# Hybrid decoder layer: all of GpSimd's DMA additions for weight sums issued in the projections, whole, at 0.75 for each weight load, and none beside the attention pairs

## The chip, the cores and the metric

The kernel runs on one core of a Trainium2 chip. Its time is the device time of one execution in microseconds (us). The engines go by the profile's names: PE is TensorE (matmuls; PEld is its weight loading), DVE is VectorE, ACT is ScalarE, POOL is GpSimd, SP is SyncE, which here only issues DMAs.

## The reference

One layer of a decoder trunk, in float32: an RMS norm, one wide input projection whose columns feed three token mixers (gated DeltaNet, GLA, forgetting attention), SiLU gates on each, one output projection with a residual, and a last norm.

```python
def hybrid_layer(x, norm_w, w_in, ...):
    h = rms_norm(x, norm_w)
    proj = (jnp.pad(h, ((0, 0), (PAD, 0), (0, 0))) @ w_in)      # 2048 -> 7585 columns
    (dq, dk, dv, dz, db, da, gq, gk, gv, gz, gl, fq, fk, fv, fz, ff) = split_cols(proj)
    o_dn = gated_head_norm(gated_delta_rule_chunked(...), dz, dn_norm_w)    # 6 heads x 128
    o_gla = gated_head_norm(gla_chunked(...), gz, gla_norm_w)               # 5 heads
    o_fox = forgetting_attention(fq, fk, fv, log_f) * silu(fz)              # 5 heads x 128
    return x + jnp.concatenate([o_dn, o_gla, o_fox], -1) @ w_out
```

There are 512 tokens and 16 meta tokens (528 in all), and the model is 2048 wide.

## The kernel before, in words

**Projections.** Each block of 128 output columns has a weight of 2048 x 128, which is loaded in two halves of 128 x 1024 (512 KB). `load_half` (L144) issues the load on SP's queue into `raw`; ACT casts it to a high part `whi` (L170), DVE subtracts to get the low part `wlo` (L171), and PE multiplies `whi` with the high and low parts of the activations and `wlo` with the high part (L245). `raw`, `whi` and `wlo` have two buffers each, so the loads run about two halves ahead of PE. Blocks come in the order: DeltaNet group 0 (keys, values, queries), DeltaNet group 1, GLA gates, GLA heads, the first attention head; between them stand the small matmuls of the mixers, placed in PE's order by hand.

**Pairs.** For attention heads 1 to 4 most blocks are computed two at a time, by `inproj_pair`: a Strassen-Winograd scheme with seven products (L580) in place of eight. It needs sums and differences of weights. The output projection of the first ten heads does the same in its products (L1410).

**Weight sums by DMA.** The sums are made in DRAM scratch, `ti` (seven input pairs) and `tw` (five output pairs), by DMAs alone. For each pair four copies ("moves") put a weight half into scratch: one move goes out on SP's queue in each `load_half` behind the weight load (L149). Then four additions per pair, DMAs with `accum_op=add` that GpSimd issues, add another weight or an earlier sum to it. Twelve pairs make 48 moves and 48 additions. Additions are generators in the list `chores`: first two for each pair that add a weight to a move (`ti<-in_w_in`, `tw<-in_w_dn`), then one for each pair that adds sum 0 to copy 1, then one that adds sum 1 to copy 3 (`ti<-ti`, `tw<-tw`); the input pairs come before the output pairs. How many go out is set in `load_half`:

```python
        due[0] += rate[0]                  # L156; due starts at -6
        while due[0] > 0 and chores:
            cost = next(chores[0], None)   # issues one addition (or half of one)
            if cost is None:
                chores.pop(0)
            else:
                due[0] -= cost
```

`AHEAD` (L1294) sets the rate. From the first DeltaNet block on it is 0.55 additions for each weight half. At attention head 1, where the pairs begin, it becomes 0.26, and there an addition is cut into two halves of 64 partitions (L494), each with a semaphore wait for the newest `wlo` subtraction on DVE; in the projections it is whole (L499) and only ordered behind the newest cast.

**Order.** A scheduler sets each engine's order when the program is built, from these dependencies and priorities. POOL's queue also holds the clamp of every SiLU (L390), the masks (L702, L726, L1225), memsets and products of the mixers, and 24 loads of the activations for the pairs (L535, L536, L555). An instruction on POOL starts only when all ahead of it have been issued.

**The inverse of a DeltaNet group** (`dn_inverse`) is a chain that passes POOL and three DMA trips: POOL clears `ab` (L739), ACT's queue loads it from scratch (L747, L748), POOL sets its diagonal (L751), DVE does 58 dependent steps (L756, L758), ACT's queue writes it out (L761, L762) and loads it turned (`iv`, L765, `xm`, L767), DVE transposes blocks (L771), and PE multiplies (`pm`, L777) at a place that is fixed in its order. ACT copies the transposed blocks into `uf`, which POOL clears at L793.

Of the kernel before, what the change touches and what calls it, by code (L numbers as in the profile page):

```python
# [14 lines left out]
ALU = mybir.AluOpType  # L15
# [3 lines left out]
P = 128  # L19
# [63 lines left out]
def tile_hybrid_trunk(ctx, tc, xT, xtok, mtok, w_gate, w_in, w_out, w_dn, consts, lmask, fin_w, out, dbg=None):  # L83
# [19 lines left out]
    V, A, G, PE = nc.vector, nc.scalar, nc.gpsimd, nc.tensor  # L103
# [71 lines left out]
    pace, splits, heads_, waits = [None, None], [], [], []  # L175

    def paced(*ins):

        for x in ins:
            tc.add_manual_dep(x.ins, pace[x.ins.engine == pace[1].engine].name, mybir.DependencyInfo(  # L180
                mybir.DependencyClass.NoSync, mybir.DependencyReason.DATA), reason="paced")
# [16 lines left out]
    def part(name, n=512):  # L198
        return hp.tile([P, T], F32R, tag="x", name=name)[:, :n]
# [29 lines left out]
    head = {}  # L229
# [259 lines left out]
    def steps_of(jobs):  # L489

        for out_, in_ in jobs:
            if ("pair", 0) in head:
                for s in (slice(0, 64), slice(64, P)):
                    x = G.dma_start(out=out_[s], in_=in_[s], accum_op=ALU.add, max_dma_last_dim=2048)  # L494
                    tc.add_manual_dep(x.ins, pace[1].name, mybir.DependencyInfo(
                        mybir.DependencyClass.Sync, mybir.DependencyReason.DATA), reason="paced")
                    yield 0.5
            else:
                paced(G.dma_start(out=out_, in_=in_, accum_op=ALU.add, max_dma_last_dim=2048))  # L499
                yield 1  # L500

    def in_jobs(n):
        h, one, two = PAIRS[n]
# [11 lines left out]
    def jobs(*groups):  # L515

        for g_ in groups:
            moves.extend(dict(out=o, in_=i) for o, i in g_[0])
        for st in range(1, 4):
            for g_ in groups:  # L520
                chores.append(steps_of(g_[st]))
# [769 lines left out]
            nc.sync.dma_start(out=zd[DN_HEADS + GLA_HEADS + h], in_=z)  # L1291


    AHEAD = {(0, -1): (0.55, (-1, -2, -3, -4, -5, -6, -7), (0, 1, 2, 3, 4)), ("f", 1): (0.26,)}  # L1294
    XSUM = {1: (0, 1, 2), 2: (3, 4, 5), 3: (6, 7)}
    MIX = 10
    PM, SP = (308, 340), (8, 11)
# [1 line left out]
    def ahead(g, i):  # L1299
        for n in AHEAD.get((g, i), ()):  # L1300
            if isinstance(n, tuple):
                jobs(*[in_jobs(-k - 1) if k < 0 else out_jobs(k) for k in n])
            else:
                rate[0] = n
# [133 lines left out]
    def weigh(tb, cc):  # L1438
        return G.tensor_tensor(out=acc[tb, cc], in0=acc[tb, cc], in1=fw[cc], op=ALU.mult)  # L1439
# [119 lines left out]
    for c in range(4):  # L1559
        f = part(f"fw{c}").bitcast(F32)  # L1560
# [16 lines left out]
    for cc in range(3):  # L1577
        for tb in range(4):
            x = weigh(tb, cc)
# [4 lines left out]
    for tb in range(4):  # L1584
# [25 lines left out]
        for cc in (1, 0, 3, 2):  # L1610
# [5 lines left out]
            else:  # L1616
                V.tensor_scalar_mul(a, a, r)
            (nc.scalar if tb == 3 and cc == 2 else nc.sync).dma_start(
                out=out[tb * P : (tb + 1) * P, cc * 512 : (cc + 1) * 512], in_=a)
# [60 lines left out]
```

## Time and profile before

| | |
|---|---|
| median of 3 runs | 987.03 us (986.32 to 987.07) |
| the profiled execution | 986.87 us, its span 985.2 us, 1.67 us outside it |
| granted TensorE clock | 0.997 |
| busy in the span | PE 975.0 us, DVE 670.5, ACT 480.3, POOL 218.2 |

Busy times come from the instructions' records; a wait is put down to the instruction that ended it. "L499" is line 499 of the kernel before. A row of the DMA list gives the issuing queue, how often, the size, and the median time from issue to landing.

### The profile page before, as it was taken

To read this page: it belongs to the slowest core of one execution; us is meant where nothing else is said; L and a number is where in the kernel's file an instruction comes from. 1 tells how busy PE (TensorE), PEld (TensorE's weight loads), DVE (VectorE), ACT (ScalarE), POOL (GpSimd) and SP (SyncE) were. 2 spreads that over 40 slices of the span, in tenths; PEclk is the share of its full clock that TensorE was granted. 3 is DMA by queue.
4 is the path that set the end of the run, shared out by engine and by line. 5 is a ranking of instruction groups with operands and counts; after the bars stand their busy time and mean duration, and the time that the engine had idled before them with its cause. 6 is when DMAs were issued, how large, how long until landed. Compare 5 with 4: busy or idle time off the path is not lost.

```text
span 985.2 us, 19830 instructions
## 1 busy us (share of the span) xinstructions
PE 975.0 (99%) x7762; PEld 894.4 (91%) x7762; DVE 670.5 (68%) x1462; ACT 480.3 (49%) x1051; POOL 218.2 (22%) x237
## 2 busy tenths in 40 slices
PE   9999999999999999999999999999999999999996
PEld 7899999899999888899899988899999998888885
DVE  5457886975657985334685847867767768987665
ACT  7753534344456334234546445655555545644345
POOL 0021322222123334201213122333322120000033
PEclk9999999999999999999999999999999999999998
DMA  9835598887458787644646666677766588366534
GB/s 345 303 119 206 161 251 222 238 257 224 127 164 221 212 252 191 164 112 102 154 138 161 158 153 194 190 218 218 195 200 171 174 267 296 132 214 212 186 115 172
DMA packets 70339, 191.83 MB, mean 195 GB/s; under 512 B 14077, under 2 KB 17325, under 8 KB 69476
## 3 DMA queue, kind: packets, MB, share of 16 engines
q1 hardware_dynamic: 46048, 152.53, 45.2%
q0 software_dynamic: 15104, 31.66, 18.4%
q10 hardware_dynamic: 9092, 6.36, 2.4%
q8 instruction: 61, 1.00, 0.4%
q14 instruction: 34, 0.28, 0.1%
HBM read 179.84 MB, written 60.88 MB: 244 GB/s over the span
## 4 chain that ended last, share of the span: by engine, by line
PE 98%; DVE 1%; ACT 1%; issue 0%; POOL 0%; DVEq 0%; ACTq 0%; POOLq 0%
PE pp L245 49%; PE pp_a L580 8%; PE pq L1410 6%; PE pp L314 5%; PE pa L1410 3%; PE ps L1410 3%; PE pt L1410 2%; PE pp_b L580 2%; PE pp_d L580 2%; PE pp_c L580 2%; PE pr L1410 1%; PE pss L1059 1%; PE pgate L431 1%; PE pfo L1285 1%; PE pfa L1237 1%; PE pg L723 1%
## 5 line engine op out<-in xcount | busy, mean ns | idle before, releaser
L245 PE MATMUL pp<-xl,whi 128*128 128x264 f32 (+2 forms) x1120 | 273.9, 306 | 0.0
L245 PE MATMUL pp<-xh,whi 128*128 128x264 f32 (+2 forms) x1120 | 272.9, 306 | 0.0
L245 PE MATMUL pp<-xh,wlo 128*128 128x264 f32 (+2 forms) x1120 | 272.2, 305 | 0.0
L170 ACT CAST whi<-raw 128x1024 fp32r<-128x1024 f32 x131 | 137.2, 1047 | 180.2 <-PE pp L245 125.1
L171 DVE TENSOR_TENSOR wlo<-raw,whi 128x1024 fp32r<-128x1024 f32 x131 | 162.8, 1243 | 66.4 <-ACT whi L170 56.0
L245 PEld LDWEIGHTS pp<-xl,whi 128*128 128x128 f32 x1120 | 182.7, 189 | 9.1 <-issue 0.4
L245 PEld LDWEIGHTS pp<-xh,whi 128*128 128x128 f32 x1120 | 182.3, 189 | 9.2 <-issue 0.2
L245 PEld LDWEIGHTS pp<-xh,wlo 128*128 128x128 f32 x1120 | 182.8, 189 | 8.5 <-issue 0.2
L390 POOL TENSOR_SCALAR stc<-cv 128x528 f32<-128x528 f32 (+1 forms) x18 | 28.1, 1563 | 145.8 <-DVE cv L622 136.2
L622 DVE SCALAR_TENSOR_TENSOR cv<-pb,cpk,cv 128x528 f32<-128x528 f32 (+1 forms) x54 | 41.1, 760 | 0.8
L1439 POOL TENSOR_TENSOR acc<-acc,fw 128x512 f32<-128x512 f32 x4 | 6.1, 1542 | 138.9 <-DVE wll L171 138.9
L170 ACT CAST whis<-raws 128x1024 fp32r<-128x1024 f32 x20 | 20.7, 1049 | 28.0 <-PE ps L1410 9.7
L171 DVE TENSOR_TENSOR wlos<-raws,whis 128x1024 fp32r<-128x1024 f32 x20 | 24.2, 1222 | 14.8 <-ACT whis L170 14.8
L580 PE MATMUL pp_a<-t,whi 128*128 128x264 f32 (+1 forms) x224 | 30.3, 283 | 0.0
L580 PEld LDWEIGHTS pp_a<-t,whi 128*128 128x128 f32 x224 | 28.0, 188 | 0.4
L580 PE MATMUL pp_a<-xh,whi 128*128 128x264 f32 x112 | 28.1, 286 | 0.0
L580 PE MATMUL pp_a<-xl,whi 128*128 128x264 f32 x112 | 27.9, 285 | 0.0
L379 DVE TENSOR_TENSOR pb<-pp,rstd 128x264 f32<-128x264 f32 (+1 forms) x36 | 13.8, 421 | 17.3 <-PE pp L245 17.3
L1410 PE MATMUL pq<-whia,a 128*128 128x512 f32 x80 | 25.4, 393 | 0.0
L1410 PE MATMUL ps<-whis,s 128*128 128x512 f32 x80 | 25.4, 394 | 0.0
L1410 PE MATMUL pq<-whis,s 128*128 128x512 f32 x80 | 25.4, 394 | 0.0
L390 POOL TENSOR_SCALAR stdz<-zdz 128x512 f32<-128x512 f32 x6 | 11.2, 1877 | 63.2 <-DVE zdz L408 62.2
(506 smaller groups left out, 2111.4 us busy)
## 6 DMA issues: line engine op xcount, KB each, us to landing
raw<-in_w_in SPq DMA_DIRECT2D x103, 512.0 KB, 3.6
ti<-in_w_in SPq DMA_DIRECT2D x28, 512.0 KB, 5.3
raw<-ti SPq DMA_DIRECT2D x28, 512.0 KB, 3.7
tw<-in_w_dn SPq DMA_DIRECT2D x20, 512.0 KB, 5.2
raws<-tw SPq DMA_DIRECT2D x15, 512.0 KB, 4.3
ti<-in_w_in POOLq DMA_DIRECT2D x14, 512.0 KB, 6.0
ti<-ti POOLq DMA_DIRECT2D x14, 512.0 KB, 7.0
tw<-in_w_dn POOLq DMA_DIRECT2D x10, 512.0 KB, 6.9
```

Of the source, the lines that this page charges most:

```text
L170: pace[0] = A.copy(hi, raw).ins
L171: pace[1] = V.tensor_tensor(out=lo, in0=raw, in1=hi.bitcast(F32), op=ALU.subtract).ins
L245: mm = PE.matmul(p_[:, :nt], wt[:, j * m : (j + 1) * m], xx[k][:, t0 : t0 + nt], start=(k == 0 and wt is hi and xx is xh), stop=(k == KT - ...
L314: mm = PE.matmul(ps[:, :S], wt[:, j * P : (j + 1) * P], xx[k][:, NM:T], start=(k == 0 and wt is hi and xx is xh), stop=(k == KT - 1 and wt ...
L379: V.tensor_tensor(out=o, in0=p_[rows], in1=rstd[rows, t0 : t0 + n], op=ALU.mult)
L390: maxes.append(G.tensor_scalar_max(t, src, LOW).ins)
L431: PE.matmul(pgate[a][:, :HT], wg[k // 8][:, k % 8, :], xx[k][:, a * HT : (a + 1) * HT], start=(k == 0 and xx is xh), stop=(k == KT - 1 and ...
L580: m = PE.matmul(p_[:, cols], wt[:, j * P : (j + 1) * P], xx[j][part_][:, cols], start=first and i == 0, stop=i == len(todo) - 1, skip_grou ...
L622: V.scalar_tensor_tensor(out=c, in0=pb[:, t0 + w : w + T], scalar=cwc[:, blk, w : w + 1], in1=c, op0=ALU.mult, op1=ALU.add)
L723: PE.matmul(pg[:r, j * r : (j + 1) * r], kT[:, j, ts], kT[:, j, ts], start=True, stop=True)
L1059: mm = PE.matmul(ps[o0 : o0 + n, b * n : b * n + n], kx[rr, k0 : k0 + n], qx[rr, q0 : q0 + n], start=True, stop=True)
L1410: mm = PE.matmul(p_, o_[:, s], w_, start=(first and n == 0), stop=(last and n == 2), skip_group_check=True)
```

## The change

The branch of `steps_of` that cuts an addition in two beside the pairs goes; every addition is whole and only ordered, not made to wait. The rate is 0.75 from the first DeltaNet block on, and the rate for the pairs is gone.

```diff
     def steps_of(jobs):
         for out_, in_ in jobs:
-            if ("pair", 0) in head:
-                for s in (slice(0, 64), slice(64, P)):
-                    x = G.dma_start(out=out_[s], in_=in_[s], accum_op=ALU.add, max_dma_last_dim=2048)
-                    tc.add_manual_dep(x.ins, pace[1].name, mybir.DependencyInfo(
-                        mybir.DependencyClass.Sync, mybir.DependencyReason.DATA), reason="paced")
-                    yield 0.5
-            else:
-                paced(G.dma_start(out=out_, in_=in_, accum_op=ALU.add, max_dma_last_dim=2048))
-                yield 1
+            paced(G.dma_start(out=out_, in_=in_, accum_op=ALU.add, max_dma_last_dim=2048))
+            yield 1
...
-    AHEAD = {(0, -1): (0.55, (-1, -2, -3, -4, -5, -6, -7), (0, 1, 2, 3, 4)), ("f", 1): (0.26,)}
+    AHEAD = {(0, -1): (0.75, (-1, -2, -3, -4, -5, -6, -7), (0, 1, 2, 3, 4))}
```

The order of PE's instructions is the same in both programs; those of SP, ACT and DVE differ by two or three instructions that change places with a neighbour. POOL's order differs throughout. Lines behind L500 are seven lower in the changed kernel (L499 is L492 there).

POOL around the inverse of DeltaNet group 0, before (`stc` and `stdz` are SiLU clamps, `ab` the inverse's buffer):

```order
L390 TENSOR_SCALAR stc_1652<-cv_1647 128x528
L499 DMA ti<-in_w_in 256x512
L390 TENSOR_SCALAR stc_1792<-cv_1787 128x512
L739 MEMSET ab_2052 51x1024
L499 DMA ti<-in_w_in 256x512
L390 TENSOR_SCALAR stc_1919<-cv_1914 128x512
L751 MEMSET ab_2052 51x32
L499 DMA ti<-in_w_in 256x512
```

The same place now:

```order
L390 TENSOR_SCALAR stc_1654<-cv_1649 128x528
L492 DMA ti<-in_w_in 256x512
L390 TENSOR_SCALAR stc_1795<-cv_1790 128x512
L492 DMA ti<-in_w_in 256x512
L732 MEMSET ab_2056 51x1024
L492 DMA ti<-in_w_in 256x512
L390 TENSOR_SCALAR stc_1922<-cv_1917 128x512
L744 MEMSET ab_2056 51x32
L492 DMA ti<-in_w_in 256x512
```

One more addition stands ahead of the memset of `ab`.

POOL some 40 us later, before (`stdz` the clamp of a gate, `uf` the inverse's result, `pb` a border of the convolution, `b` a block buffer of the inverse):

```order
L390 TENSOR_SCALAR stdz_2705<-zdz_2703 128x512
L617 MEMSET pb_2712 128x3
L499 DMA ti<-in_w_in 256x512
L793 MEMSET uf_2212 128x1536
L390 TENSOR_SCALAR stc_2834<-cv_2829 128x528
L617 MEMSET pb_2840 128x3
L805 MEMSET b_2220 64x384
L499 DMA ti<-in_w_in 256x512
```

The same place now:

```order
L390 TENSOR_SCALAR stdz_2709<-zdz_2707 128x512
L610 MEMSET pb_2716 128x3
L492 DMA ti<-in_w_in 256x512 x2
L786 MEMSET uf_2216 128x1536
L390 TENSOR_SCALAR stc_2838<-cv_2833 128x528
L610 MEMSET pb_2844 128x3
L492 DMA ti<-ti 256x512
L798 MEMSET b_2224 64x384
```

Two additions stand ahead of the memset of `uf` (the last two that add an input weight to a move), and one ahead of the memset of `b`.

POOL at the first pair and its attention head, before (`vf`, `zfz`, `fqk` hold values, gate, and queries and keys of a head; `fcm` is a mask):

```order
L494 DMA tw<-tw 128x512 x2
L1204 TENSOR_TENSOR vf_7767<-vf_7767,rstd 128x528
L494 DMA tw<-tw 128x512
L1266 COPY fs_7821<-vf_7258 128x128
L1205 TENSOR_TENSOR zfz_7769<-zfz_7769,rstd 128x512
L1225 AFFINE_SELECT fqk_8130<-fqk_8130 128x128
L494 DMA tw<-tw 128x512
L1225 AFFINE_SELECT fcm_8137<-fqk_7467 128x384
L494 DMA tw<-tw 128x512
L1272 CAST ptm_7879<-zero_c 128x512
```

The same place now:

```order
L1197 TENSOR_TENSOR vf_7775<-vf_7775,rstd 128x528
L1259 COPY fs_7829<-vf_7272 128x128
L1198 TENSOR_TENSOR zfz_7777<-zfz_7777,rstd 128x512
L1218 AFFINE_SELECT fqk_8136<-fqk_8136 128x128
L1218 AFFINE_SELECT fcm_8143<-fqk_7479 128x384
L1265 CAST ptm_7887<-zero_c 128x512
```

The halved additions are gone from there, and POOL has no DMA left beside the pairs.

## Prediction

> **What bounds the kernel now.** I read the page first: busy times, the clock, the DMA queues and the chain of work that ended last.
>
> ```profile
> span 985.2 us, 19830 instructions
> ...
> PE 975.0 (99%) x7762; PEld 894.4 (91%) x7762; DVE 670.5 (68%) x1462; ACT 480.3 (49%) x1051; POOL 218.2 (22%) x237
> ...
> PEclk9999999999999999999999999999999999999998
> ...
> PE 98%; DVE 1%; ACT 1%; issue 0%; POOL 0%; DVEq 0%; ACTq 0%; POOLq 0%
> ```
>
> PE is busy 975.0 of 985.2 us at the full clock, and 98% of the chain is PE. The next question is whether PE waits anywhere, so I asked for PE's waits:
>
> ```profile
> PE warm L309 <- POOL ones L114: 1.2, 1, 1.2
> PE pss L1059 <- issue: 0.5, 1, 0.5
> ```
>
> That is all: 1.2 us at the start and 0.5 us of instruction issue. No wait on a weight, on GpSimd or on a DMA is left to remove. The change touches neither the matmuls nor PE's order. It can win only what is hidden inside busy time, and lose if a delay becomes longer than its cover. Two views bound these: the stretches of the program, and the additions themselves.
>
> ```profile
> 98.50:123.10 24.60, 24.60 (x209) 24.38 (x209) 19.70 (x49) 12.97 (x49) 8.01 (x12) 1.00 0.54 160
> 123.10:221.70 98.60, 98.60 (x773) 94.20 (x772) 78.37 (x172) 36.83 (x50) 27.15 (x27) 1.00 0.87 242
> ...
> 640.40:747.00 106.60, 106.60 (x861) 104.85 (x860) 75.75 (x190) 58.34 (x122) 34.33 (x36) 1.00 0.76 205
> 747.00:805.00 58.00, 58.00 (x467) 56.91 (x466) 40.50 (x92) 31.51 (x61) 10.43 (x8) 1.00 0.59 187
> ```
>
> The columns are length, then PE, PEld, DVE, ACT and POOL busy with their counts, the clock, and the DMA engines' share. The DMA share is 0.87 in the projections from 123 to 222 us, where copies and additions run together, and 0.76 in the pairs that have half additions (640 to 747).
>
> ```profile
> L499 POOL DMA_DIRECT2D ti<-in_w_in x14: 932/946/1117, 114.6 to 277.0; - x14
> ...
> L499 POOL DMA_DIRECT2D tw<-tw x2: 1004/1323/1642, 584.0 to 617.9; - x2
> ```
>
> ```profile
> L494 POOL DMA_DIRECT2D tw<-tw x16: 806/822/897, 642.5 to 744.6; - x16
> ```
>
> A whole addition holds POOL 0.95 us, a half one 0.82 us. The two whole `tw<-tw` and the sixteen halves are the last ten of the 48.
>
> **Part 1, the pairs.** Sixteen half issues go, 16 x 0.82 = 13 us of POOL, beside work on which PE never waits. POOL's own waits there go too:
>
> ```profile
> POOL tw L494 <- DVE wlo L171: 31.5, 7, 7.0
> ```
>
> The halves stood 31.5 us waiting for `wlo`, and with them what is queued behind on POOL: `vf`, `zfz` and `fqk` times `rstd`, masks, a clamp. All of that now comes earlier, and no one waited for it long enough to stop PE. What could be hidden in PE's busy time shows in the same matmuls with half additions beside them (first fence) and without (second):
>
> ```profile
> L580 PE MATMUL pp_a<-xh,wlo 128*128 128x264 f32 x64 | 10.1, 290 | 0.0
> ...
> L580 PE MATMUL pp_b<-xh,whi 128*128 128x264 f32 x32 | 8.1, 288 | 0.0
> ```
>
> ```profile
> L580 PE MATMUL pp_a<-xh,wlo 128*128 128x264 f32 x40 | 6.8, 295 | 0.0
> ...
> L580 PE MATMUL pp_b<-xh,whi 128*128 128x264 f32 x16 | 4.0, 284 | 0.0
> ```
>
> One mean falls by 4 ns and the other rises by 5 ns. If all 861 matmuls of the stretch won the 4 ns, it would be 3.4 us; if they all lost 5 ns, 4.3 us. With both signs in two rows I take 0 and keep a gain of 3.4 us for the range.
>
> **Part 2, POOL in the projections.** The rule due = -6 + 0.75 n lets addition number k (from 0) out at the first n above (k + 6) / 0.75, in place of 0.55: the first after 9 weight halves in place of 11, the 48th after 71. The last stands, in POOL's order, right behind the product of the third GLA pair,
>
> ```profile
> 535.84 1.30 POOL L1021 TENSOR_TENSOR gpr<-gqk 64x512 f32<-64x512 f32 x1 [3.20 <-DMA gqk<-gqk]
> ```
>
> so at about 537 us, not 745. Between 98 and 222 us there are 15 in place of 10. Five more issues are 5 x 0.95 = 4.8 us of POOL, which is busy 8.0 + 27.2 of 123 us there: nothing by itself. It matters where POOL is a step of a chain, and that is the inverse of DeltaNet group 0.
>
> ```profile
> 159.92 0.94 POOL L739 MEMSET ab<- 51x1024 f32 x1
> 160.82 1.05 POOL L499 DMA_DIRECT2D ti<-in_w_in  x1
> ...
> 170.41 0.15 POOL L751 MEMSET ab<- 51x32 f32 x1 [3.17 <-DMA ab<-scmeta]
> ...
> 198.37 0.95 POOL L499 DMA_DIRECT2D ti<-in_w_in  x1
> 198.98 1.74 POOL L793 MEMSET uf<- 128x1536 f32 x1
> 210.99 1.53 POOL L390 TENSOR_SCALAR stc<-cv 128x528 f32<-128x528 f32 x1 [10.28 <-DVE cv L622]
> ```
>
> One addition now stands ahead of the memset of `ab` (159.92), so the load into `ab`, the diagonal (170.41) and DVE's dependent steps start 1.05 us later. The chain comes back to PE here:
>
> ```profile
> 214.66 0.58 DVE L771 STREAM_TRANSPOSE iv<-iv 128x384 f32<-128x384 f32 x1 [0.81 <-DMA iv<-sc]
> ```
>
> ```profile
> 219.99 0.95 PE L777 MATMUL pm<-iv,an 32*32 32x32 f32 x48
> ```
>
> The transposes end at 215.2 and PE reads them at 219.99: a cover of 4.8 us. A delay of 1.05 us costs nothing.
>
> The two additions that now stand back to back at 198.4 need moves that are only just issued (the last one at 197.42):
>
> ```profile
> 197.42 0.49 SPq L149 DMA_DIRECT2D ti<-in_w_in  x1
> ```
>
> ```profile
> raw<-in_w_in SPq DMA_DIRECT2D x17, 512.0 KB, 4.2
> ti<-in_w_in SPq DMA_DIRECT2D x15, 512.0 KB, 6.7
> ti<-in_w_in POOLq DMA_DIRECT2D x9, 512.0 KB, 7.1
> tw<-in_w_dn SPq DMA_DIRECT2D x2, 512.0 KB, 9.1
> ab<-scr ACTq DMA_DIRECT2D x1, 192.0 KB, 5.7
> iv<-sc ACTq DMA_DIRECT2D x1, 192.0 KB, 5.2
> ```
>
> These are landings between 123 and 222 us. The move lands 6.7 us after its issue, at 204.1, or at 206.5 with the longest median of the list, 9.1 us. POOL stands still for that time. Queued behind are the memset of `uf` and the clamp `stc`, and behind that `pb` and `b`. The memset then ends at 204.1 + 0.95 + 1.74 = 206.8 us (209.2 at worst); `stc` has its data only at 210.99, and `uf` is not written before the transposes have ended. Cost 0; without that cover, up to 206.5 - 198.4 = 8.1 us.
>
> **Part 3, the DMA engines.** Between 123 and 222 us three more additions run.
>
> ```profile
> q1 hardware_dynamic: 2932, 17.59, 50.5%
> q0 software_dynamic: 2448, 4.72, 30.9%
> ```
>
> GpSimd's queue (q0) takes 30.9% of 98.6 us for nine additions, so one takes 3.4 us of all 16 engines. Three more make 0.87 x 98.6 + 10.2 = 96.0 us of 98.6, a share of 0.97: nearly full, not over. Who would feel it first? The weight loads. Without any addition (49 to 98 us) a load lands after
>
> ```profile
> raw<-in_w_in SPq DMA_DIRECT2D x6, 512.0 KB, 3.2
> ```
>
> 3.2 us, and with additions in flight 9 x 7.1 = 64 of 98.6 us, after 4.2 us. With twelve, in flight 85 of 98.6 us, I estimate 3.2 + 1.0 x 85 / 64 = 4.5 us. What stands against that is the time to the cast:
>
> ```profile
> 186.18 0.33 SPq L147 DMA_DIRECT2D raw<-in_w_in  x1
> ```
>
> ```profile
> 194.06 1.05 ACT L170 CAST whi<-raw 128x1024 fp32r<-128x1024 f32 x1 [3.62 <-PE pp L245]
> ```
>
> Loads run two halves ahead, so the one issued at 186.18 is cast at 194.06, 7.9 us later, and the cast waits for PE to give back the `whi` buffer, not for data. A load may land 3.7 us later than now before anything moves. The estimate of 0.3 us costs nothing. The extra DMA trips in the chain of part 2 (5.7 and 5.2 us) grow at the same rate by about a tenth, some 1.1 us, with the 1.05 us together 2.2 of the cover of 4.8 us.
>
> At this place a rule can be weighed. The Trainium skill, "DMA: Bandwidth & Descriptors", section on queues, rings and completion order, says that each DMA engine takes turns, packet by packet, between the queues that have work. By that rule a second addition lines up behind the first in GpSimd's queue and the loads keep their turn, so a load would stay near 4.2 us and the sum would be the same; it speaks against the first rival below more than the rows do, which show only 3.2 and 4.2.
>
> After 222 us the share is lower and the additions no denser than one for 1.33 weight halves.
>
> **Sum.** Pairs 0, POOL 0, chain 0, DMA 0: span 985.2 us, with the 1.67 us outside it 986.9. The median of the runs, 987.03, is 0.16 above this execution, so I predict **987.0 us**. A difference of 0.2%, 2 us, is about what a measurement of this kernel can tell from no change.
>
> **The rivals.**
> *The inverse's chain outlasts its cover* (slower). Three DMA trips of group 0 (load of `ab`, write of `sc`, load of `iv`) meet a DMA share of 0.97. For it: the chain is the only place where POOL and DMA trips lead in series to a fixed place on PE, and DVE already stops 0.81 us there. Against it: 4.8 us of cover. It decides when the delays sum to more than 4.8 us. If the two loads, 5.7 and 5.2 us, and a write that I put at as much as the shorter of them take half as long again, that is 8.1 + 1.05 - 4.8 = 4.3 us: 991.3. Chance 0.25.
> *The DMA engines become the bound* (slower). If the additions' time between 123 and 222 us displaced loads one for one, as at a share of 1, the three would cost up to 10.2 us; with the 2.6 us that are idle taken off, 7.6: 994.6. For it, 0.97; against it, 3.7 us of cover for each load. Chance 0.12.
> *The pairs hide a gain* (faster): the 3.4 us of part 1 in full, 983.6, because `wlo` and the products on POOL come sooner and the small pauses between matmuls close. For it, the 31.5 us of waits on POOL that go; against it, the rows with opposite signs and a PE that shows no wait there. Chance 0.13.
> That the change does not do what it says is excluded by POOL's order, in which no addition stands beside the pairs.
>
> **How the numbers follow.** No change has 0.50, the rivals 0.25, 0.12 and 0.13. Faster by over 0.2%: 0.13; within 0.2%: 0.50; slower: 0.37. The forecast's own range is 986 to 988.5. For 8 in 10 I reach up to the second rival's 994.6, rounded down to 994 since half of its cases lie below, and down to 985.0, which leaves out most of the gain: about 0.1 below and 0.06 above.
>
> **What would show it.** Right: PE's waits again only at the start and at `pss`; the last GpSimd addition near 537 us; the DMA share between 123 and 222 us near 0.97; the memset of `ab` about 1 us later; `pm` at 220.0 us; loads landing in 4 to 5 us. Wrong: a wait of PE at `pm` or of `whi` on a DMA (slower), or the stretch of the pairs, 106.6 us from the first half addition's place to the last, shorter by 2 us or more (faster).

## The result, and the profile after

The changed kernel takes 993.92 us (median of 4 runs, 991.02 to 995.2) against 987.05 us (986.32 to 987.6) for the kernel before: the ratio is 1.0064, 95% interval 1.0051 to 1.0077. It is slower by 0.64%, where the prediction had "no change". The profiled execution takes 993.54 us, its span is 991.8 us, 6.6 us more than before. Lines behind L500 are seven lower than in the rows of before.

The page of after, with the busy times and the chain that ended last:

```profile
PE 976.9 (98%) x7762; PEld 893.5 (90%) x7762; DVE 668.6 (67%) x1462; ACT 480.6 (48%) x1051; POOL 213.5 (22%) x229
...
PE 86%; DVE 5%; DMA 4%; ACT 2%; issue 2%; POOL 1%; SPq 0%; ACTq 0%; DVEq 0%; POOLq 0%
```

PE is busy hardly longer, but its share of the chain falls from 98% to 86%: DVE, DMA and ACT now lie on it. PE's waits in after (who was waited for, us in total, times, longest; the 1.2 us at `warm` stands in both kernels):

```profile
PE pp L245 <- DVE wlo L171: 1.6, 3, 0.7
PE pp L245 <- ACT whi L170: 1.3, 2, 0.9
PE pss L1052 <- ACT kq L1061: 1.3, 1, 1.3
...
PE pss L1052 <- DVE kq L1038: 0.5, 1, 0.5
```

Before had only the two rows `warm` and `pss`. Where the waits lie is found by setting PE's 7762 instructions of both traces side by side (their order is the same) and taking the start in after less the start in before. This lag is 0.2 us at 205 us and grows at three places: by 2.7 us between 217 and 235 us (the inverse of DeltaNet group 0, "first place" below), by 2.2 us between 344 and 350 us (the inverse of group 1, "second place"), and by 2.1 us between 561 and 568 us (the scores of the third GLA pair, "third place"); an issue pause of 0.7 us at 511 us of before is not there in after. In between, and from 580 us to the end, it is flat.

The same stretches as in the prediction, and the pairs' stretch at its place in after (length, then PE, PEld, DVE, ACT and POOL busy, clock, DMA share, GB/s):

```profile
98.50:123.10 24.60, 24.60 (x209) 24.38 (x208) 19.17 (x50) 12.15 (x48) 12.04 (x15) 1.00 0.83 218
123.10:221.70 98.60, 98.06 (x758) 93.41 (x759) 73.76 (x163) 33.71 (x45) 29.43 (x29) 1.00 0.92 247
...
647.00:753.60 106.60, 106.60 (x861) 104.84 (x860) 75.73 (x189) 58.30 (x122) 19.00 (x20) 1.00 0.50 167
```

The pairs take 106.6 us for 861 matmuls, as before. **First place**, POOL and then ACT in after (a bracket is the idle time of the engine before the row, and what ended it):

```profile
160.74 1.32 POOL L732 MEMSET ab<- 51x1024 f32 x1
...
171.90 0.15 POOL L744 MEMSET ab<- 51x32 f32 x1 [3.97 <-DMA ab<-scmeta]
...
205.47 0.88 POOL L492 DMA_DIRECT2D ti<-in_w_in  x1 [4.64 <-DMA ti<-in_w_in]
...
214.06 0.94 POOL L492 DMA_DIRECT2D ti<-ti  x1
```

```profile
208.47 0.32 ACTq L754 DMA_DIRECT2D sc<-ab  x1
...
213.99 0.39 ACTq L758 DMA_DIRECT2D iv<-sc  x1
...
216.24 1.05 ACT L170 CAST whi<-raw 128x1024 fp32r<-128x1024 f32 x1 [9.29 <-issue]
...
223.16 1.05 ACT L170 CAST whi<-raw 128x1024 fp32r<-128x1024 f32 x1
```

The same rows of ACT's queue before:

```profile
206.94 0.32 ACTq L761 DMA_DIRECT2D sc<-ab  x1
...
209.41 0.39 ACTq L765 DMA_DIRECT2D iv<-sc  x1
...
211.55 1.05 ACT L170 CAST whi<-raw 128x1024 fp32r<-128x1024 f32 x1 [4.80 <-PE pp L245]
```

The load of `iv` cannot be issued before the write of `sc` has landed. That took 2.5 us before and 5.5 us after, with the addition of 205.47 in flight; the load itself, up to the transposes, took 5.2 and then 6.5 us, with the one of 214.06. While ACT's queue stands at the load, a weight cast stands behind it: 216.24 for 211.55. The chain comes back to PE here (DVE's transposes, then PE's `pm`):

```profile
220.45 0.58 DVE L764 STREAM_TRANSPOSE iv<-iv 128x384 f32<-128x384 f32 x1 [1.90 <-DMA iv<-sc]
```

```profile
218.60 0.51 PE L245 MATMUL pp<-xh,wlo 128*128 128x264 f32 x2 [0.39 <-DVE wlo L171]
...
221.08 0.95 PE L770 MATMUL pm<-iv,an 32*32 32x32 f32 x48
...
232.99 0.52 PE L245 MATMUL pp<-xh,whi 128*128 128x264 f32 x2 [0.43 <-ACT whi L170]
...
234.42 0.39 PE L245 MATMUL pp<-xh,wlo 128*128 128x264 f32 x1 [0.68 <-DVE wlo L171]
```

The transposes are 5.8 us later than before, and `pm` starts 1.1 us later: the cover of 4.8 us is gone. But `pm` itself costs only 0.2 of the 2.7 us. 0.7 us is lost ahead of it, at the weight half whose cast stood behind the load (218.60), and 1.7 us behind it, at a half whose cast and subtraction come late (232.99 and 234.42): ACT has by then waited 1.87 us (0.72 before) for the transposes at its first copy into `uf`, and the casts and SiLU steps that lead there stand behind the copies. **Second place**, ACT's queue, before and then after:

```profile
330.13 1.89 ACTq L742 DMA_DIRECT2D scr<-an  x4
...
334.26 0.32 ACTq L747 DMA_DIRECT2D ab<-scr  x1
335.69 1.05 ACT L170 CAST whi<-raw 128x1024 fp32r<-128x1024 f32 x1 [5.79 <-DVE vpm L838]
341.81 1.05 ACT L170 CAST whi<-raw 128x1024 fp32r<-128x1024 f32 x1 [5.07 <-PE pp L245]
```

```profile
333.00 3.03 ACTq L735 DMA_DIRECT2D scr<-an  x4
...
344.31 0.32 ACTq L740 DMA_DIRECT2D ab<-scr  x1
344.67 2.00 ACT L170 CAST whi<-raw 128x1024 fp32r<-128x1024 f32 x2 [12.18 <-PE pp L245]
```

The load of `ab` waits for the write of `scr`: issued 2.2 us behind its end before, 8.3 us after, and two casts wait behind it. In after three additions are issued at 325.0, 329.3 and 330.8 us, just ahead of the write; before there was one, at 326.7. **Third place**: ACT's load of `fqk` waits for a store from the buffer that it takes over (SP's queue, then ACT's, in after):

```profile
544.53 0.32 SPq L1145 DMA_DIRECT2D zd<-gqk  x1
```

```profile
552.62 0.34 ACTq L1214 DMA_DIRECT2D fqk<-gd  x1
```

From store to load it is 8.1 us; before it was 5.7 us (539.89 to 545.61). A gate step of the third GLA pair and a cast stand behind the load.

### The profile page after: what moved, and what is told of

Its sections match the earlier page's. It is cut to its first block, busy times and chain, and to the rows that moved or that the text cites. A ratio compares the mean times of both kernels' runs of the same rounds, so it can differ in the third digit from the quotient of the medians.

```text
span 991.8 us, 19815 instructions
## 1 busy us (share of the span) xinstructions
PE 976.9 (98%) x7762; PEld 893.5 (90%) x7762; DVE 668.6 (67%) x1462; ACT 480.6 (48%) x1051; POOL 213.5 (22%) x229
## 4 chain that ended last, share of the span: by engine, by line
PE 86%; DVE 5%; DMA 4%; ACT 2%; issue 2%; POOL 1%; SPq 0%; ACTq 0%; DVEq 0%; POOLq 0%
PE pp L245 38%; PE pp_a L573 8%; PE pq L1403 6%; PE pp L314 4%; PE pa L1403 3%; PE ps L1403 3%; PE pt L1403 2%; PE pp_b L573 2%; PE pp_d L573 2%; PE pp_c L573 2%; PE pr L1403 1%; PE pss L1052 1%; DMA ab<-scmeta 1%; DMA zd<-gqk 1%; PE pgate L431 1%
```

## The experiments

The theories: **A**, an addition in flight lengthens a short DMA trip on which ACT's queue waits (A1: PE loses through the casts queued behind; A2: through the inverse's late results). **B**, the density of additions over the whole stretch counts. **C**, GpSimd's own time: the issue ahead of the memset of `ab` and the wait for a move. The table gives the medians and, for each kernel's one profiled run, by how much PE's lag against before grows at the three places. A ratio is against runs of before made beside that kernel (medians 987.1 to 987.8 us), so kernels are best compared by their ratios. Line numbers of these kernels differ from after's by a few lines.

| kernel | median, us | ratio to before, 95% | first | second | third |
|---|---|---|---|---|---|
| after | 993.92 | 1.0051 to 1.0077 | 2.7 | 2.2 | 2.1 |
| e1_pairs_whole | 988.8 | 0.9998 to 1.0015 | 0.1 | 0.0 | 1.7 |
| e2_hold | 987.45 | 0.9985 to 1.0002 | 0.1 | 0.0 | 0.0 |
| e3_narrow | 987.21 | 0.9983 to 1.0 | 0.1 | 0.0 | 0.0 |
| e4_phase | 990.52 | 1.0019 to 1.0041 | 0.1 | 0.0 | 0.0 |
| e5_casts_first | 995.76 | 1.0063 to 1.0088 | 8.1 | 0.0 | 1.0 |
| e6_burst | 993.26 | 1.0038 to 1.0062 | 0.0 | 5.1 | 0.0 |
| e7_packets_1k | 994.98 | 1.0048 to 1.0079 | 5.1 | 2.5 | 2.4 |
| e8_packets_4k | 994.81 | 1.0057 to 1.0095 | 2.4 | 2.5 | 1.7 |
| e9_burst_casts_first | 987.08 | 0.9989 to 1.0007 | 0.1 | 0.0 | 0.0 |
| e10_second_casts_first | 991.89 | 1.0028 to 1.0053 | 3.0 | 0.0 | 1.1 |
| e11_one_addition | 987.7 | 0.9989 to 1.0007 | 0.1 | 0.0 | 0.5 |
| e12_hold_third | 993.2 | 1.0044 to 1.0071 | 2.0 | 1.2 | 0.1 |
| e13_fast_to_25 | 988.28 | 0.9994 to 1.0014 | 0.1 | 0.0 | 1.9 |
| e14_fast_to_26 | 989.56 | 1.0002 to 1.0031 | 4.3 | 0.0 | 0.0 |
| e15_fast_to_27 | 990.85 | 1.002 to 1.0045 | 3.3 | 0.0 | 0.0 |

**One part alone: whole additions beside the pairs.**

```diff
-    AHEAD = {(0, -1): (0.75, ...)}
+    AHEAD = {(0, -1): (0.55, ...), ("f", 1): (0.26,)}
```

> One part of the change alone: the additions beside the pairs are whole and only ordered, at the rates of the kernel before (0.55, then 0.26). In the trace of after PE's lag behind before no longer grows once the pairs begin (6.5 us at 580 us and at the end), so both theories say 987.0 us, within 1. If whole additions beside the pairs cost something of their own, or the loss of the halves gains something, the stretch of the pairs is longer or shorter than the 106.6 us of before by over 1 us.

988.8 us: same within its interval. The lag of 1.7 us at the third place is there although the additions up to it are those of before, so this place also loses in runs without the change's additions. In the pairs two small waits of 0.5 and 0.4 us appear, and PE's lag grows there by 1.6 us: by the measure set above (1 us) whole additions beside the pairs did cost something of their own in this run. The change has none there, so this is no part of its loss.

**Hold the additions back at three places.**

```diff
+        nth[0] += 1
+        left = 0 if nth[0] in HOLD else CAP    # HOLD = 26, 27, 41 to 44, 70 to 72; CAP = 1
-        while due[0] > 0 and chores:
+        while due[0] > 0 and chores and left > 0:
...
+                left -= cost
```

> The changed kernel with the same additions at 0.75, but none is issued at nine weight halves (numbers 26, 27, 41 to 44, 70 to 72), which lie beside the trips of both inverses and the store before the first attention head; at most one goes out for each half, so that they are made up for behind each gap. Theory A (an addition in flight lengthens a short DMA trip on which ACT's queue waits, with casts queued behind): the three places of loss, 2.7, 2.2 and 1.9 us, go, 987 to 988 us. Theory B (the density of additions over the whole of the projections): as after, 993 to 994 us. Theory C (GpSimd's own time for issues ahead of the memset of ab, and its wait for a move): about 0.5 to 1 us of the first place goes at most, 992 to 994 us.

987.45 us, as theory A has it: all of the loss is gone at the same mean rate, and B falls. Of C, the extra issue ahead of the memset of `ab` is still there, but the wait for a move is only 1.5 us, so that half of it is left to the next run. Besides the waits of before PE has one, of 0.3 us. The two trips in ACT's queue:

```profile
207.76 0.32 ACTq L759 DMA_DIRECT2D sc<-ab  x1
...
210.31 0.39 ACTq L763 DMA_DIRECT2D iv<-sc  x1
...
330.12 1.90 ACTq L740 DMA_DIRECT2D scr<-an  x4
...
333.34 0.32 ACTq L745 DMA_DIRECT2D ab<-scr  x1
```

The write of `sc` takes 2.6 us again and the wait for `scr` 1.3 us.

**Narrow additions.** `in_[:, :128]` and `out_[:, :128]` in each addition.

> The changed kernel with each addition cut to its first 128 of 1024 columns: every sum lacks seven eighths of its additions. GpSimd issues as many additions in nearly the same places and waits for the same moves, but the DMA engines have an eighth of the bytes to add. Theories A and B: the loss goes, 986 to 988 us. Theory C (GpSimd's issues and its wait): the loss at the first inverse stays, 990 us or more.

987.21 us. This kernel leaves out seven eighths of each addition. With GpSimd's issues kept, and still 3.3 us of its wait for a move, nothing is lost: C falls, it is the additions' DMA work, not GpSimd's time.

**Another phase.** The count starts at -6.5.

> The changed kernel with the count started at -6.5 in place of -6: the rate stays 0.75 and the number the same, but the weight half without an addition is another one of each four (26, 30, ..., 42 in place of 28, 32, ..., 44), so no addition is issued between about 199 and 214 us, and one fewer stands ahead of the memset of ab. Theory A: the write and load of the first inverse take about 2.5 and 5.2 us as before, and the first loss of 2.7 us goes; at the second inverse two additions in place of three stand ahead of the scratch write, about half of 2.2 us goes; the third place as after: 990 us. Theory B: 993 to 994 us as after. Theory C: between the two, with the gain at the first place only.

990.52 us, near the forecast in the median, but the runs lie from 988.25 to 993.25, and the profiled one (988.58) loses at no place. Which places the longer runs lose at was not profiled.

**Casts ahead of ACT's waits.** The waiting loads are ordered behind the casts (numbers from 0).

```diff
+        if g == 1:
+            waits.append((x.ins, 43, casts))     # x: the load of ab
...
+        if g == 0:
+            waits.append((x.ins, 26, casts))     # x: the loads of iv and xm
...
+            if g == 0:
+                waits.append((x.ins, 27, casts)) # x: the copies into uf
```

> The changed kernel with the same additions; only ACT's order differs at the two inverses: the loads that wait for a write (iv and xm of group 0, ab of group 1) stand behind the weight casts that followed them, and the copies into uf of group 0 behind the next cast. The DMA trips stay as long as in after. Theory A1 (PE loses because casts stand behind ACT's wait): the 2.2 us at the second inverse and most of the 2.7 us at the first go, the third place stays, about 990 us. Theory A2 (PE loses because the inverse's own results come late): as after, 993 to 994 us.

995.76 us: the sum missed, and the two places part. At the second the lag grows by 0.0 us: A1 holds there. At the first it grows by 8.1 us in place of 2.7: the trips became longer still (write of `sc` 6.1 us, load of `iv` 9.4), and the chain itself reaches PE at `pm` (PE, then the clock behind it):

```profile
225.81 1.49 PE L778 MATMUL pm<-iv,an 32*32 32x32 f32 x48 [5.07 <-DVE iv L772]
```

```profile
226.00:232.00 6.00, 6.00 (x69) 5.94 (x66) 5.52 (x10) 2.81 (x6) 0.17 (x1) 0.50 0.34 113
```

PE waits 5.1 us, and then runs at a granted clock of 0.50 for 6 us, which costs 3 us more. So A2 can hold at the first place: with the casts out of the way the late chain reaches PE directly. In after that part is 0.2 us.

**A burst in the kernel before, and the cure on top.**

```diff
+        nth[0] += 1
+        due[0] += {42: 1, 43: 1, 44: -1, 47: -1}.get(nth[0], 0)
```

> The kernel before with two additions pulled forward to the weight halves 42 and 43, just ahead of the scratch write of the second inverse (and two fewer behind it); the rate stays 0.55 elsewhere and the halves beside the pairs stay. Theory A: ACT's queue waits some 5 to 8 us for that write in place of 2.2, and PE loses about 2 us there and nothing elsewhere: 989 to 990 us. Theory B (the density over the whole): no change, 987 to 988 us.

993.26 us, more than forecast (989 to 990). Two additions moved by some 16 us are enough for a loss nearly as large as that of the whole change (1.0050 against 1.0064). ACT's queue, PE's waits and the window behind them:

```profile
330.00 2.67 ACTq L745 DMA_DIRECT2D scr<-an  x4
...
342.86 0.32 ACTq L750 DMA_DIRECT2D ab<-scr  x1
343.22 2.00 ACT L173 CAST whi<-raw 128x1024 fp32r<-128x1024 f32 x2 [13.44 <-DMA scr<-an]
```

```profile
PE pp L248 <- ACT whi L173: 2.4, 1, 2.4
...
PE pp L248 <- DVE wlo L174: 0.5, 1, 0.5
```

```profile
344.00:349.00 5.00, 4.16 (x10) 3.05 (x11) 4.67 (x11) 1.22 (x2) 0.82 (x2) 0.67 0.64 242
```

2.9 us are waits; most of the rest of the 5.1 us is the clock behind them, 0.67 over these 5 us.

> The kernel before with the same two additions pulled forward to the halves 42 and 43, and in addition ACT's load of ab at the second inverse ordered behind the two weight casts that stood behind it. The DMA trip stays long. Theory A1 (casts behind ACT's wait): the loss of the burst alone, 5.6 us against its before, goes: 987 to 988.5 us. Theory A2 (the inverse's results late, or the DMA engines full): 992 to 993 us.

987.08 us: the same burst with the load of `ab` behind the two casts costs nothing, though the write of `scr` still takes 10.3 us from issue to landing (11.6 in e6, 2.9 in before; here ACT's queue):

```profile
329.91 3.62 ACTq L747 DMA_DIRECT2D scr<-an  x4
...
337.48 1.05 ACT L175 CAST whi<-raw 128x1024 fp32r<-128x1024 f32 x1 [7.78 <-PE pv L840]
341.60 1.05 ACT L175 CAST whi<-raw 128x1024 fp32r<-128x1024 f32 x1 [3.07 <-PE pp L250]
341.86 0.32 ACTq L752 DMA_DIRECT2D ab<-scr  x1
```

That settles the second place: A1. The same order of ACT in the changed kernel, at the second inverse alone:

> The changed kernel with that same order of ACT at the second inverse alone; the first inverse and the store of the third GLA pair are as in after. Theory A1: the 2.2 us of the second place go, 991 to 992 us, with the shift of PE flat between 240 and 500 us. Theory A2: 993 to 994 us.

991.89 us, 2.0 us less than after, and no lag at the second place.

**Packets of another size** (`max_dma_last_dim` of 1024 and 4096).

> The changed kernel with the additions in packets of 1 KB in place of 2 KB. If the trips wait until the additions in flight have drained (the total time of an addition counts), nothing is won: 993 to 995 us, more if the smaller packets make an addition longer. If the size of the packet that stands ahead of a small packet counts, the waits halve: about 990 us.

> The changed kernel with the additions in packets of 4 KB in place of 2 KB. If the total time of an addition counts: 992 to 994 us, less if fewer packets make it shorter. If the size of the packet that stands ahead of a small one counts, the waits double: 998 us or more.

994.98 and 994.81 us: the packet's size hardly counts. That the trips end when the additions ahead have drained would fit, but these two runs do not show it.

**The first place, addition by addition, in the kernel before.** First, one addition pulled forward: `due[0] += {26: 1, 28: -1}.get(nth[0], 0)`.

> The kernel before with one addition pulled forward, to the weight half 26, so that two are in flight from about 199 us on when DVE's chain of the first inverse ends at 207 us; the move it needs has landed long before, so GpSimd does not wait. Theory A: the write of sc takes 4 to 5.5 us in place of 2.4, the cast behind it is late and PE loses 1 to 2.7 us at 218 to 232 us: 988.5 to 990 us. Theory C (GpSimd's wait for a move and its issue ahead of the memset of ab make the loss): 987 to 988 us.

987.7 us. The write of `sc` took 4.5 us (issued 207.5, `iv` 212.0) as expected, but PE lost nothing: my loss of 1 to 2.7 us was wrong, one longer trip fits the cover. Then the changed kernel's additions up to a given half:

```diff
+        due[0] += 0.75 if nth[0] <= FAST else rate[0]      # FAST = 25, 26, 27
+        due[0] -= 0.2 * FAST if nth[0] == FAST + 1 else 0
```

> The kernel before with the rate of 0.75 up to weight half 25 and then no addition until the count of 0.55 has caught up, 0.55 from there. GpSimd's order up to 200 us is that of after (the addition ahead of the memset of ab too), but none is issued near the write of sc or the load of iv. If the issues ahead of the memset of ab alone cost time: over 988.5 us. If the trips count: the transposes end about 1.5 us later than in before, within their cover of 4.8 us, and the time is 987 to 988 us.

> The same up to half 26: one addition more, for which GpSimd waits until its move has landed (about 205 us), and which is in flight during the write of sc. Write of sc about 5.5 us, load of iv about 5.2 us: the transposes end some 4.5 us later than in before, just within the cover: 987 to 988.5 us. If GpSimd's wait makes the loss, the whole 2.7 us is here: 990 us.

> The same up to half 27: one addition more, issued at about 214 us, in flight during the load of iv. The transposes end some 5.8 us later than in before, 1 us beyond the cover, and casts come late behind ACT's waits and copies: 2.7 us at the first place and nothing elsewhere, 989.5 to 990.5 us. If only the write of sc counts, it equals the run up to half 26.

988.28, 989.56 and 990.85 us: each addition nearer to the trips adds about 1.3 us to the median; the intervals of neighbours overlap, those of the first and the third do not. The first is the same as before within its interval and loses nothing at the first place, though it has the extra issue ahead of the memset of `ab`: GpSimd's share is nothing by itself. With the second the runs spread from 985.99 to 992.78 us. The profiled one, 992.76, loses 4.3 us there, by one wait of 2.3 us for a cast that stood behind the loads of `iv` and `xm`, and a clock of 0.57 over the 4 us behind it; the fastest can have lost none. With the third the shortest run is 989.22 us. In its profile the transposes end 7.3 us later than in before (5.8 expected; DVE's steps alone end 3.1 us later), and still PE does not wait at `pm`. Its waits between 200 and 240 us:

```profile
PE pp L248 <- DVE wlo L174: 1.2, 2, 0.7
PE pp L248 <- ACT whi L173: 0.9, 2, 0.5
```

So at the first place, too, PE loses at casts and subtractions behind ACT's waits. The late chain has a part in it, through the copies into `uf`; how the loss divides between the two is not shown.

**The last two additions held back.** `HOLD` is 70 to 72, with no cap.

> The changed kernel with only the last two additions held back, behind the store of the third GLA pair's first head (halves 70 to 72 without one). Theory A: the two inverses lose as in after, and the third place's 1.9 us goes at most: 991.5 to 993 us. Theory B: as after, 993 to 994 us.

993.2 us. From store to load it is now 3.3 us, and the lag at the third place 0.1 us. The gain of 0.7 us in the median is not clear of the noise, and smaller than the 2.1 us of after's profile: that place loses in some executions and not in others (1.7 and 1.9 us in two kernels with the additions of before there, 0.0 in others).

No kernel with the whole sums is faster than before beyond its interval: PE's waits there are 1.7 us in all, so there is nothing for the changed rate to win.

## Why the prediction was wrong, by its own steps

*Part 1, the pairs: 0.* Right. 861 matmuls take 106.6 us with the halves and without; the lag is 6.53 us at 640 us and 6.55 us at 747 us. The rival of a hidden gain (983.6) has no place.

*Part 2, POOL.* Nearly right in its terms: the memset of `ab` 0.8 us later, the diagonal 1.5 us (1.05 forecast), the wait for a move until 205.5 us (forecast 204.1), the last addition at 541.8 us, which is 537.2 less the lag. None of it reaches PE by itself (e13, e3).

*Part 3, the DMA share.* 0.92, not 0.97; weight loads land in 4.9 us, not 4.5, inside their cover of 3.7 us. That the DMA engines become the bound (994.6) is near the time by accident: e2 has the same additions at the same rate and 987.45 us.

*The failed step* is the sentence "The extra DMA trips ... grow at the same rate by about a tenth, some 1.1 us". It scaled two trips, the loads of `ab` and `iv`, and put the write of `sc` at nothing without a reason. That write grew by 3.0 us, the load of `iv` by 1.2, the load of `ab` not at all (5.5 us for 5.7), and DVE's chain came 1.5 us late: 5.8 us against a cover of 4.8, where the step had 2.2. An average over the stretch stood in for what happens to one trip: in before the write of `sc` fell into a gap between two additions (198.4 and 212.9 us), so the rows could not show how a trip fares beside one.

The first rival named this place and its threshold (delays beyond 4.8 us), and it did count the write. e15 gives 990.85 us for this place alone, beside its 991.3, but that nearness is partly luck. It had PE waiting 4.3 us at `pm`; PE waited 0.15 us there in after and not at all in e15, and lost its time at casts.

*Two steps were missing*, and they carry most of the loss. The chain was called "the only place where POOL and DMA trips lead in series to a fixed place on PE". But the waiting engine is ACT, whose queue runs in order: what counts at the second place is the cast behind a waiting load, at the first such a cast too (2.4 of 2.7 us are lost at `whi` and `wlo`), and this was not costed. And "after 222 us ... the additions no denser than one for 1.33 weight halves" took the count for the time: POOL issued three within 6 us, just ahead of the scratch write of group 1. The third place is of another kind: there the addition goes out 2.7 us ahead of the store in after and 2.8 us in before, so its 2.1 us cannot be put down to the change.

*The rule on turns.* Rows first: packets of GpSimd (q0), SP (q1) and ACT (q10) at the second place in after, from 337 to 338 and from 339 to 341 us, and ACT's in 1 us of before, beside only 7 packets of GpSimd:

```profile
q0 software_dynamic: 100, 0.20, 107.9%
q10 hardware_dynamic: 99, 0.01, 16.5%
```

```profile
q1 hardware_dynamic: 120, 0.84, 100.2%
...
q10 hardware_dynamic: 119, 0.02, 4.9%
```

```profile
q10 hardware_dynamic: 1054, 0.13, 82.7%
```

ACT's 128-byte packets of `scr` go at 1054 in 1 us when nearly alone, and one for one beside the additions' packets of 2 KB, later beside those of SP's queue. The Trainium skill, "DMA: Bandwidth & Descriptors", section on queues, rings and completion order, says that engines alternate packet by packet, and these rows agree. The prediction used that rule only for the weight loads, which it protects; a write of 1536 tiny packets it holds back to about one for each packet of the queue beside it, be that the additions' or SP's.

Turns are not the whole of it. The first packet of `sc` moves 0.8 us after its issue in before and 3.2 us after it in after, which is 2.4 of the 3.0 us by which this write grew (for `scr` 1.2 and 3.5 us). GpSimd's queue is the busy one in that time. In after, from 209 to 211 us, ACT's queue has no packet, and in before, from 207.4 to 209.4 us, it has 70 (after, then before):

```profile
q0 software_dynamic: 114, 0.23, 75.9%
```

```profile
q10 hardware_dynamic: 70, 0.21, 43.3%
```

Why the first packet comes so late is not shown.

## What to carry to other kernels

Before moving background DMAs, list every short DMA trip on which a queue waits in order, and what stands behind that wait; an average share of the DMA engines says nothing about them. Keep background DMAs out of those stretches, or order the waiting load behind the work that PE needs next: either took the whole loss away at the second place. At the first, where the chain behind the load comes back to PE, the new order made the loss larger (e5), and keeping the additions out is what helped (e2). When a trace shows a trip with nothing beside it, its duration is no bound for the same trip with company.

## What was not expected of the hardware

A wait of PE costs more than its length. Behind 2.4 and 0.5 us of waits the granted clock was 0.67 over 5 us (e6), behind 5.1 us it was 0.50 over 6 us (e5); behind waits of up to 1.3 us in after it stayed at 1.00. The length of a wait alone does not decide it: in e7 the clock was 0.50 from 237.6 to 240.9 us and the nearest waits ahead of it were only 0.2 and 0.7 us. The Trainium skill, "TensorE: Matmul & The Clock Gate", Part 1, has the half rate and an idle window of about 3.4 us before it; here less was enough.

A DMA's issue can itself hold ACT: that of `xm`, 0.93 us in before, took 5.21 us beside the additions (e5, ACT's queue):

```profile
216.22 5.21 ACTq L766 DMA_DIRECT2D xm<-sc  x1
```
